# A selective-scan loop regrouped into pairs of chunks, with its preparation moved further ahead

## The chip, the cores and the metric

The kernel runs on one core of a Trainium2 chip. The metric is the device time of one execution in microseconds (us). The engines are named as the profile names them: PE (TensorE: matmuls and transposes; PEld is its weight loading), DVE (VectorE), ACT (ScalarE), POOL (GpSimd) and SP (SyncE, which here only issues DMA transfers). Each engine executes its own instructions strictly in the order in which the program lists them; engines wait for one another through semaphores. A difference of under 0.2% (3 us here) can't be told from no change by the runs of this kernel.

## The reference: what is computed

Two layers over a sequence of 1024 tokens, each with a width of 1024. The first is a gated MLP with a causal mixing over chunks of 128 tokens. The second, which the change touches, is a Mamba-2 mixer. Cut to what matters here, with G = 8 groups of J = 4 heads, chunks of 128 tokens, head size P = 64, state size N = 128:

```
proj = h @ w_in                                   # z, x, B, C and dt
xbc  = silu(causal_conv4(x, B, C) + bias)         # 4 taps along the tokens
cs   = cumsum(dt * A)                             # within a chunk
w_ls = (C @ B.T) * exp(cs_l - cs_s) * dt_s        # causal, 128 x 128, for each head
y_diag = w_ls @ x                                 # within the chunk
states = B.T @ (exp(cs_end - cs) * dt * x)        # what a chunk adds to the state
prev_c = prev_(c-1) * exp(cs_end) + states        # carried from chunk to chunk
y_off  = (C @ prev) * exp(cs)                     # from earlier chunks
y = y_diag + y_off + x * d_skip
out = rmsnorm_by_group(y * silu(z)) @ w_out
```

## The kernel before, in words

Everything is float32; big products run as three matmuls of a split into a high and a low part (`mm3`, L131 to L136). The order of all instructions is written out by hand: under `manual_schedule` the order of the Python calls is the order on each engine.

The last third of the kernel is one loop, `scans()` (L1854). It goes over 64 pieces n = 0..63, which are 8 groups g with 8 chunks c each. Two kinds of work are woven together on PE. One is the scan itself, with small matmuls. The other is filler: `project(want(..))` takes the next units of a generator that first computes the x, B, C and z columns that the second half of the groups still needs (128x512 matmuls into the PSUM tiles `ab`) and at the end begins the output product (`bo`). One unit is six matmuls. `want` (L1881) spreads the units evenly, 2.24 a chunk, half of them after the first stretch of the chunk and half after the second.

For a chunk, PE does two stretches of small matmuls:

- `pe_b` (L1620): y_off (two 128x128 matmuls with the carried state as weights, L1626), the chunk's own contribution to the state (128x256, L1633), and y_diag (four 128x128 matmuls, L1636). The y_diag matmuls use only 64 columns of the array each: two heads share the 128 partitions of the output, and the weights are 128x64. In every fourth chunk `sum_b` (L1702) follows, which sums squares for the norm, also with 64 columns. All of these write the PSUM tiles `yy` and `sp`.
- `pe_a` for the chunk two ahead (L1593, L1594): three transposes (x in two parts, B) and C @ B.T into the tile `tp`.

Around them: `load` brings the cumulative sums of a chunk to all partitions (tile `wl`, 256 KB, SP), `decay` turns them into exp(cs_l - cs_s) on ACT (L1599, L1601), `tokens` (DVE, ACT, POOL) reads `tp` into the tile `cw`, `weights` (DVE, L1617) multiplies `wl` by C @ B.T. `update` (DVE, L1656) and `carry` (POOL, L1647) form the state, `out` and `gate` the result. `queue` holds the steps of the convolution over the filler's products (one ACT pass, three DVE passes L1322 and a Silu for each `ab` tile); `drain()` runs one of them, once a chunk.

Half of the groups (0, 1, 3 and 5, `SPILT`) had their x, B, C computed earlier; they lie in DRAM as `xbc_d` and come back in halves of four chunks (1 MB each) through `prefetch` (L1549), which also loads z and exp(cs) (tile `ze`). SP issues all those transfers in program order, so a transfer waits behind the one before it. `prefetch(g, 1)` is called at the end of chunk 1 of group g, `prefetch(g + 1, 0)` at the end of chunk 5. The sums of squares go to DRAM through `sum_c` (`ss_d<-gsq`), called at the end of chunks 0 and 4, a chunk after `sum_b`.

PSUM has eight banks of 128x512; the `ab` tiles take four of them, and `yy`, `sp`, `tp` share the other four.

Of the kernel before, what the change touches and what calls it, by code (L numbers as in the profile page):

```python
# [11 lines left out]
ALU = mybir.AluOpType  # L12
# [3 lines left out]
P = 128  # L16
# [6 lines left out]
G = 8  # L23
# [6 lines left out]
def kernel(  # L30
# [21 lines left out]
    nc = tc.nc  # L52
# [1344 lines left out]
    def projections():  # L1397

        seq = [(g, kind) for g in plain for kind in ("x", "bc")] + [(G - 1, "z")]
        raw, W = {}, {}  # L1400

        def cols(g, kind):
            return ((g * 256, g * 256 + P) if kind == "z" else (DI + g * 256, DI + g * 256 + P) if kind == "x"
                    else (2 * DI + g * P, 2 * DI + 1024 + g * P))

        def load(i, kh):
            if i < len(seq):
                c = cols(*seq[i])
                r = slice(kh * 512, (kh + 1) * 512)
                raw[i, kh] = load_raw([b_w_in[r, k:k + P] for k in c] if seq[i][1] == "bc" else  # L1410
                                      [b_w_in[r, c[0]:c[0] + 256]], 4)

        def prep(i, kh):
            if i < len(seq):
                W[i, kh] = wh([P, 4, 256]), wl([P, 4, 256])
                split(*W[i, kh], raw.pop((i, kh)), nc.gpsimd if i else V)
                load(i + 1, kh)

        def push(g, kind, m, a):
            if m == 0:  # L1420
                sts[g][kind] = s8([P, 2, T], kind)
            if kind == "z":
                queue.append([lambda: nc.scalar.activation(sts[g][kind][:, m, :], a.rearrange("p a b -> p (a b)"),
                                                           AF.Silu)])
                return 1
            ops = conv_ops(sts[g][kind][:, m, :], a.rearrange("p a b -> p (a b)"), (cols(g, kind)[m] - DI) // P)
            n = len(queue)
            ops = [[o] for o in ops]
            if queue:
                queue[-1] += ops.pop(0)  # L1430
            queue.extend(ops)
            if m == 1:
                queue.append([lambda: nc.scalar.activation(sts[g][kind], sts[g][kind], AF.Silu)])
            return len(queue) - n

        for kh in range(2):
            load(0, kh)
        yield
        for kh in range(2):
            prep(0, kh)  # L1440
            yield
        last = 0
        for i, (g, kind) in enumerate(seq):
            for m in range(2):
                drain(len(queue) - last)
                ab = acc2("ab")
                for kh in range(2):
                    for th in (1, 0):
                        for k in range(4):
                            mm3(ab[:, th, :], [w[:, k, m * P:(m + 1) * P] for w in W[i, kh]],  # L1450
                                [h_[:, k, :] for h_ in H2[f"A{2 - th}{kh + 1}"]], kh == 0 and k == 0,
                                kh == 1 and k == 3)
                            if (kh, th, k) == (1, 0, 3):
                                last = push(g, kind, m, ab)
                            if k % 2:
                                yield
                    if (m, kh) == (0, 1):
                        prep(i + 1, 0)
                    elif (m, kh) == (1, 0):
                        prep(i + 1, 1)  # L1460
# [85 lines left out]
    ss_d = dr.tile([G, T], F32, name="ss_d")  # L1546
    rs_d = dr.tile([G, T], F32, name="rs_d")

    def prefetch(g, th):  # L1549

        st = sts[g]
        if g in xbc_d:
            t = st["xbc", th] = s8([P, 4, 512], "xbc")
            nc.sync.dma_start(out=t, in_=xbc_d[g][:, th])
        ze = st["ze", th] = s8([P, 4, 512], "ze")
        if g < G - 1:
            nc.sync.dma_start(out=ze[:, 0:2], in_=z_d[g][:, :, th * 512:(th + 1) * 512])
# [6 lines left out]
    class Scan:  # L1564


        def __init__(self, g, eng):
            self.g, self.st, self.eng = g, sts[g], eng
            self.wl, self.tp, self.cw, self.ps, self.state = {}, {}, {}, {}, {}
            if g < G - 1:  # L1570
                gd.append(dr.tile([P, 2, T], F32, name=f"g_d{g}"))
            else:
                gd.append(self.st["x"])
# [43 lines left out]
            V.tensor_tensor(out=wl, in0=wl, in1=self.cw[c][:, 640:768].unsqueeze(1).broadcast_to([P, 4, P]),  # L1617
                            op=ALU.mult)

        def pe_b(self, c, ends=None):  # L1620

            w, wl = self.cw[c], self.wl.pop(c)
            yy = sm("yy")
            if c > 0:
                for pt in range(2):
                    nc.tensor.matmul(out=yy[:, 256 + pt * P:384 + pt * P],  # L1626
                                     lhsT=self.state[c - 1][:, pt * P:(pt + 1) * P], rhs=self.x(3, c),
                                     start=True, stop=True)
            sp = None
            if c < 7 or ends is not None:  # L1630
                sp = sm("sp")
            if c < 7:
                nc.tensor.matmul(out=sp[:, 0:256], lhsT=w[:, 512:640], rhs=w[:, 256:512], start=True, stop=True)  # L1633
            for j in range(4):
                pt, f = j // 2, j % 2
                nc.tensor.matmul(out=yy[f * 64:(f + 1) * 64, pt * P:(pt + 1) * P], lhsT=w[:, j * 64:(j + 1) * 64],  # L1636
                                 rhs=wl[:, j, :], start=True, stop=True)
            if ends is not None:
                ends.sum_b(sp[:, 256:512], 2 if ends.g == G - 1 else 1)
            self.ps[c] = yy, sp  # L1640

        def carry(self, c):

# [7 lines left out]
        def update(self, c):  # L1651
            if c == 0:
                self.state[0] = k1([P, 256], "state")
                V.tensor_copy(out=self.state[0], in_=self.ps[0][1][:, 0:256])
            elif c < 7:
                V.tensor_tensor(out=self.state[c], in0=self.ps[c][1][:, 0:256], in1=self.state[c], op=ALU.add)  # L1656

        def y(self, c):

# [1 line left out]
                return self.z(c)  # L1661
            return self.cw[c][:, 768:1024].rearrange("p (m l) -> p m l", m=2)

        def out(self, c):
            yy, t2 = self.ps.pop(c)[0], self.y(c)
            if c > 0:
                t1 = k1([P, 2, P], "t1")
                V.tensor_tensor(out=t1, in0=yy[:, 256:512].rearrange("p (m l) -> p m l", m=2),
                                in1=self.st["ze", c // 4][:, 2:4, c % 4 * P:c % 4 * P + P], op=ALU.mult)
            for pt in range(2):  # L1670
                V.scalar_tensor_tensor(t2[:, pt, :], self.x(pt, c), dsk[:, 2 * self.g + pt:2 * self.g + pt + 1],
                                       yy[:, pt * P:(pt + 1) * P], ALU.mult, ALU.add)
            if c > 0:
                self.eng.tensor_tensor(out=t2, in0=t2, in1=t1, op=ALU.add)

        def gate(self, c):
# [173 lines left out]
    def scans():  # L1850
# [27 lines left out]
                    scan[g] = Scan(g, nc.gpsimd)  # L1878
                getattr(scan[g], f)(c, *a)

        prefetch(0, 0)  # L1881
        project(AHEAD // 2 + 1)
        while todo or late:
            convolve()
        for n in range(2):
            at("load", n)
        drain(1)
        for n in range(2):
            at("decay", n)
        drain(len(queue))  # L1890
        at("pe_a", 0), at("tokens", 0), at("weights", 0)
        drain(len(queue))
        project(AHEAD)
        at("pe_a", 1), at("tokens", 1), at("weights", 1)
        at("load", 2)
        for n, (g, c) in enumerate(chunks):
            if n == M + 3:
                drain(len(queue))
# [4 lines left out]
                end["scan"] = scan[G - 1]  # L1903
                bo.get("b", 0, 0, 0)
            p = g if c >= 4 else g - 1
            at("pe_b", n, scan[p] if c % 4 == 3 and p >= 0 else None)
            project(want(n + .5))
            at("pe_a", n + 2)
            if n > 0:
                at("weights", n + 1)  # L1910
            at("update", n)
            at("out", n)
            at("decay", n + 2)
            at("carry", n + 1)
            drain()
            at("tokens", n + 2)
            at("gate", n)
            if n >= N - 7:
                k = n - N + 7
                if k % 2:  # L1920
                    bo.prep(1, k // 2)
                else:
                    bo.ready(0, 0, k // 2)
            at("load", n + 3)
            th = 0 if c >= 4 else 1
            if p >= 0:
                sc = scan[p]
                if p == G - 1:
                    if c == 5:
                        sc.gate_half(th), sc.squares(th)  # L1930
                elif c % 4 == 0:
                    sc.squares(th)
                elif c % 4 == 1:
                    sc.store(th)
                    sc.sum_a()
            if c % 4 == 0 and n >= 8:
                scan[g - 1].sum_c(1 - th)
            if g > 0:
                if c == 5:
                    rs[g] = group_rstd(g - 1, 0, T)  # L1940
                elif c == 6:
                    rs[g][0]()
                elif c == 7:
                    rs[g][1]()
            if c == 0 and g > 1:
                rs[g - 1][2]()
            if c == 1:
                prefetch(g, 1)
            if c == 5 and g < G - 1:
                prefetch(g + 1, 0)  # L1950
            project(want(n + 1))
        sc = scan[G - 1]
        for k in (0, 1):
            bo.get("a", 0, 1, k)
        bo.get("b", 1, 0, 0)
        sc.sum_c(0), rs[G - 1][2]()
        bo.prep(1, 3)
        sc.gate_half(1), sc.squares(1)
        end["half"] = [group_rstd(G - 1, 0, 512)]
# [61 lines left out]
```

## Time and profile before

| | |
|---|---|
| median of 3 runs | 1514.28 us (1512.39 to 1514.48) |
| the profiled execution: its own time | 1512.85 us |
| its span, first to last instruction | 1511.1 us |
| PE busy | 1471.6 us, 97% |
| DVE, ACT, POOL busy | 1053.7 (70%), 783.3 (52%), 401.5 us (27%) |
| scan loop, first to last y_diag | 1018.4 to 1350.4 us |
| granted PE clock in the loop | 1.00 |

The profile is of one execution. Matmuls overlap one another on PE, so the duration of one is longer than the distance to the next; costs are read here as the distance from the start of one group of matmuls to the start of the next. In a timeline, rows of equal matmuls are merged, "x4" being four entries; a float32 128x128 matmul leaves two entries. "Idle" time before an instruction is put down to what released it; "issue" means that nothing the profile shows was waited for.

### The profile page before, as it was taken

What the parts mean: (1) busy time and instruction counts of PE and PEld (TensorE: products, weight loads), DVE (VectorE), ACT (ScalarE), POOL (GpSimd) and SP (SyncE); (2) the same over time, 40 slices, a digit from 0 to 9 for tenths busy, and PEclk for the clock granted to TensorE, in tenths of its full rate; (3) what the DMA queues carried; (4) which work ended last, traced back from release to release, by engine and by line L of the source; (5) the groups of instructions that cost most, each with busy time, mean ns of one, the idle gap of its engine ahead of it and who ended that gap; (6) DMA issues with size and microseconds to landing.
All of it is one profiled execution on the core that took longest, in us unless ns stands there. A gap on an engine that the chain in (4) does not pass through costs nothing. (4 is left out here: it accounts for less than half of the span.)

```text
span 1511.1 us, 21297 instructions
## 1 busy us (share of the span) xinstructions
PE 1471.6 (97%) x7834; PEld 1222.5 (81%) x7834; DVE 1053.7 (70%) x1713; ACT 783.3 (52%) x1256; POOL 401.5 (27%) x451
## 2 busy tenths in 40 slices
PE   6899999999999999999999999999999999999997
PEld 6899988888888888877878888877777777777875
DVE  7966567665666655678666467867677787688876
ACT  6533332222323445565565566666676666756463
POOL 1111110000000023202131222217576766633121
PEclk9999999999999999999999999999999999999999
DMA  5554322322222999957377978677655565579973
GB/s 183 141 168 140 106 97 103 117 103 103 101 79 96 337 262 246 258 145 162 104 174 154 208 154 167 142 242 209 183 160 183 160 187 141 169 255 275 255 156 112
DMA packets 174952, 254.45 MB, mean 168 GB/s; under 512 B 16400, under 2 KB 103168, under 8 KB 171648
## 3 DMA queue, kind: packets, MB, share of 16 engines
q1 hardware_dynamic: 124768, 168.93, 36.0%
q0 software_dynamic: 42448, 70.27, 23.2%
q10 hardware_dynamic: 7632, 13.90, 2.6%
q8 instruction: 62, 1.02, 0.3%
q14 instruction: 42, 0.34, 0.1%
HBM read 186.14 MB, written 51.18 MB: 157 GB/s over the span
## 5 line engine op out<-in xcount | busy, mean ns | idle before, releaser
L134 PE MATMUL acc<-hh,wh 128*128 128x512 f32 x868 | 339.9, 392 | 0.9 <-ACT u L296 0.9
L136 PE MATMUL acc<-hh,wl 128*128 128x512 f32 x868 | 338.4, 390 | 2.0 <-DVE wl L112 1.8
L135 PE MATMUL acc<-hl,wh 128*128 128x512 f32 x868 | 337.9, 389 | 0.0
L112 DVE TENSOR_TENSOR wl<-wr,wh 128x1024 fp32r<-128x1024 f32 (+1 forms) x96 | 114.3, 1193 | 118.3 <-ACT wh L111 118.1
L136 PEld LDWEIGHTS acc<-hh,wl 128*128 128x128 f32 x868 | 162.9, 188 | 37.9 <-DVE wl L112 3.7
L134 PEld LDWEIGHTS acc<-hh,wh 128*128 128x128 f32 x868 | 163.1, 188 | 34.9 <-ACT u L296 1.7
L135 PEld LDWEIGHTS acc<-hl,wh 128*128 128x128 f32 x868 | 163.1, 188 | 33.1
L296 ACT COPY u<-acc 128x512 f32<-128x512 f32 x115 | 66.8, 583 | 197.8 <-PE acc L136 197.7
L111 ACT CAST wh<-wr 128x1024 fp32r<-128x1024 f32 (+1 forms) x112 | 115.2, 1030 | 94.4 <-PE acc L135 56.9
L136 PE MATMUL acc<-wh,hl 128*128 128x256 f32 x448 | 129.2, 288 | 4.1 <-DVE hl L407 3.7
L134 PE MATMUL acc<-wh,hh 128*128 128x256 f32 x448 | 129.6, 289 | 2.9 <-DVE wh L418 1.3
L135 PE MATMUL acc<-wl,hh 128*128 128x256 f32 x448 | 128.5, 287 | 1.3 <-DVE wl L421 1.3
L134 PE MATMUL ab<-hh,wh 128*128 128x512 f32 x288 | 124.7, 433 | 1.2 <-DVE zt L999 0.7
L136 PE MATMUL ab<-hh,wl 128*128 128x512 f32 x288 | 113.2, 393 | 0.0
L135 PE MATMUL ab<-hl,wh 128*128 128x512 f32 x288 | 112.7, 391 | 0.0
L136 PEld LDWEIGHTS acc<-wh,hl 128*128 128x128 f32 x448 | 87.6, 196 | 5.4 <-DVE hl L407 4.4
L134 PEld LDWEIGHTS acc<-wh,hh 128*128 128x128 f32 x448 | 87.8, 196 | 3.8 <-ACT hh L400 1.6
L135 PEld LDWEIGHTS acc<-wl,hh 128*128 128x128 f32 x448 | 87.8, 196 | 1.7 <-DVE wl L421 1.5
L1599 ACT ACTIVATE wl<-wl,tk 128x128 f32<-128x128 f32 x256 | 81.6, 392 | 3.0 <-DMA wl<-cs_d 2.7
L649 POOL DMA_DIRECT2D y_d<-y x8 | 4.4, 549 | 290.8 <-DVE y L646 290.8
L135 PE MATMUL bo<-wl,xh 128*128 128x512 f32 x192 | 75.8, 395 | 3.8 <-DVE wl L742 2.1
L112 DVE TENSOR_TENSOR wl<-t,wh 128x1024 fp32r<-128x1024 f32 (+1 forms) x38 | 45.5, 1196 | 47.5 <-ACT wh L111 47.4
(317 smaller groups left out, 3250.6 us busy)
## 6 DMA issues: line engine op xcount, KB each, us to landing
wr<-in_a_w_in_dram SPq DMA_DIRECT2D x48, 512.0 KB, 3.6
wl<-cs_d SPq DMA_DIRECT2D x64, 256.0 KB, 3.6
wr<-in_b_w_in_dram SPq DMA_DIRECT2D x30, 512.0 KB, 7.4
wb<-in_a_w_out_dram SPq DMA_DIRECT2D x10, 1024.0 KB, 11.7
wb<-in_b_w_out_dram SPq DMA_DIRECT2D x10, 1024.0 KB, 11.1
wr<-in_b_w_in_dram SPq DMA_DIRECT2D x36, 256.0 KB, 5.9
v<-v_d SPq DMA_DIRECT2D x8, 1024.0 KB, 5.1
y_d<-y POOLq DMA_DIRECT2D x8, 1024.0 KB, 5.8
```

What stands on the lines that cost most here:

```text
L111: nc.scalar.copy(out=hi, in_=src)
L112: return (eng or nc.vector).tensor_tensor(out=lo, in0=src, in1=hi.bitcast(F32), op=ALU.subtract)
L134: nc.tensor.matmul(out=o, lhsT=l[0], rhs=r[0], start=start, stop=False, **kw)
L135: nc.tensor.matmul(out=o, lhsT=l[0], rhs=r[1], start=False, stop=False, **kw)
L136: nc.tensor.matmul(out=o, lhsT=l[1], rhs=r[0], start=False, stop=stop, **kw)
L296: nc.scalar.copy(out=self.u[n][:, i], in_=a)
L649: store = lambda: nc.gpsimd.dma_start(out=y_d[-1], in_=y)
L1599: nc.scalar.activation(wl[:, j, :], wl[:, j, :], AF.Relu, scale=-1.0, bias=tokc(2, c, self.g)[:, j:j + 1])
```

## The change

The loop goes in pairs of chunks. `pe_b` is split in three: `diagonal(c)` does y_diag of both chunks c and c + 1, eight matmuls in one stretch, into one PSUM bank; `own(c)` the chunk's contribution to the state; `off(c)` its y_off, these two into a tile `os`. In an even chunk PE does own, off, then the diagonal parts of the pair, and `sum_b` behind them in every second pair; in an odd chunk only own and off. `out` is split into `skip` (adds x * d_skip to y_diag, for both chunks of the pair in the even one) and the rest.

`pe_a` and `tokens` run three chunks ahead instead of two, `weights` two ahead instead of one, `decay` three ahead. The loads of `wl` come two at a time, right behind the diagonal stretch that frees their buffers. `sum_b` moves from the last chunk of a half group to the first chunk behind it, and `sum_c` into the same chunk. `drain()` is called twice a chunk instead of once, and the first step of a new convolution is put in front of the queue's last entry instead of behind it. `prefetch` is split: the 1 MB `xbc` is asked for at the end of chunks 0 and 4, `ze` at the end of chunks 1 and 5, as before.

```diff
@@ push
             if queue:
-                queue[-1] += ops.pop(0)
+                queue[-1][:0] = ops.pop(0)
...
@@ class Scan
-        def pe_b(self, c, ends=None):
...
+        def diagonal(self, c):
+
             yy = sm("yy")
+            for e in range(2):
+                w, wl = self.cw[c + e], self.wl.pop(c + e)
+                self.yy[c + e] = yy[:, e * 256:(e + 1) * 256]
+                for j in range(4):
+                    pt, f = j // 2, j % 2
+                    nc.tensor.matmul(out=self.yy[c + e][f * 64:(f + 1) * 64, pt * P:(pt + 1) * P],
+                                     lhsT=w[:, j * 64:(j + 1) * 64], rhs=wl[:, j, :], start=True, stop=True)
+
+        def own(self, c):
+
+            w = self.cw[c]
+            if c < 7:
+                self.os[c] = sm("os")
+                nc.tensor.matmul(out=self.os[c][:, 0:256], lhsT=w[:, 512:640], rhs=w[:, 256:512],
+                                 start=True, stop=True)
+
+        def off(self, c):
+
+            if c == 7:
+                self.os[c] = sm("os")
             if c > 0:
                 for pt in range(2):
...
@@ scans
-            at("pe_b", n, scan[p] if c % 4 == 3 and p >= 0 else None)
-            project(want(n + .5))
-            at("pe_a", n + 2)
-            if n > 0:
-                at("weights", n + 1)
-            at("update", n)
-            at("out", n)
-            at("decay", n + 2)
-            at("carry", n + 1)
-            drain()
-            at("tokens", n + 2)
-            at("gate", n)
+            if c % 2 == 0:
+                at("own", n), at("off", n)
+                at("diagonal", n)
+                if c % 4 == 0 and g > 0:
+                    scan[g - 1].sum_b()
+                elif n == N - 2:
+                    scan[g].sum_b(n=2)
+                at("load", n + 4), at("load", n + 5)
+                project(want(n + .5))
+                at("pe_a", n + 3)
+                at("update", n)
+                at("carry", n + 1)
+                at("weights", n + 2)
+                at("decay", n + 3)
+                at("skip", n)
+                at("out", n)
+                at("skip", n + 1)
+                drain()
+                at("tokens", n + 3)
+                at("gate", n)
+                if c % 4 == 0 and g > 0:
+                    scan[g - 1].sum_c(1 if c else 0)
+                drain()
+            else:
+                at("own", n), at("off", n)
+                project(want(n + .5))
+                at("pe_a", n + 3)
+                at("update", n)
+                at("carry", n + 1)
+                at("weights", n + 2)
+                at("out", n)
+                drain()
+                at("decay", n + 3)
+                at("tokens", n + 3)
+                at("gate", n)
+                drain()
...
-            at("load", n + 3)
...
-            if c == 1:
-                prefetch(g, 1)
-            if c == 5 and g < G - 1:
-                prefetch(g + 1, 0)
+            k = n + 4
+            if c % 4 < 2 and k < N:
+                prefetch(k // 8, k // 4 % 2, c % 4)
             project(want(n + 1))
```

On PE, at chunk 6 of group 2 before (`yy` holds y_off and y_diag, `sp` the own part, `ab` is filler, `tp` the transposes of a later chunk):

```order
L1626 MATMUL yy<-bc,state 128x128 x2
L1633 MATMUL sp<-cw 128x256
L1636 MATMUL yy<-wl,cw 64x128 x4
L134 MATMUL ab<-hh,wh 128x512
L135 MATMUL ab<-hl,wh 128x512
L136 MATMUL ab<-hh,wl 128x512
L134 MATMUL ab<-hh,wh 128x512
L135 MATMUL ab<-hl,wh 128x512
L136 MATMUL ab<-hh,wl 128x512
L1593 MATMUL tp<-ident,xbc 128x128 x3
L1594 MATMUL tp<-xbc 128x128
```

The same chunk now, an even one (`os` holds own and y_off):

```order
L1638 MATMUL os<-cw 128x256
L1647 MATMUL os<-bc,state 128x128 x2
L1630 MATMUL yy<-wl,cw 64x128 x8
L134 MATMUL ab<-hh,wh 128x512
L135 MATMUL ab<-hl,wh 128x512
L136 MATMUL ab<-hh,wl 128x512
L134 MATMUL ab<-hh,wh 128x512
L135 MATMUL ab<-hl,wh 128x512
L136 MATMUL ab<-hh,wl 128x512
L1595 MATMUL tp<-ident,xbc 128x128 x3
L1596 MATMUL tp<-xbc 128x128
```

The stretch has eight y_diag matmuls instead of four; the transposes are those of chunk 1 of group 3 instead of chunk 0. An odd chunk has no `yy` row any more; this is chunk 1 of group 3:

```order
L1638 MATMUL os<-cw 128x256
L1647 MATMUL os<-xbc,state 128x128 x2
L134 MATMUL ab<-hh,wh 128x512
L135 MATMUL ab<-hl,wh 128x512
L136 MATMUL ab<-hh,wl 128x512
L134 MATMUL ab<-hh,wh 128x512
L135 MATMUL ab<-hl,wh 128x512
L136 MATMUL ab<-hh,wl 128x512
L1595 MATMUL tp<-ident,xbc 128x128 x3
L1596 MATMUL tp<-xbc 128x128
```

Its transposes are those of chunk 4, the first readers of the second half of `xbc`; before, they stood in chunk 2. On SP's queue, around the load of that half (before; `g_d` is a store of results, `rs_d` of norm factors, `wr` filler weights):

```order
L1709 DMA ss_d<-gsq 2x256
L1730 DMA rs_d<-rvv 128x8
L120 DMA wr<-in_b_w_in_dram 128x4x256
L1588 DMA wl<-cs_d 128x512
L1693 DMA g_d_9103<-ze 256x1x512
L1554 DMA xbc<-xbc_d_6211 128x2048
L1557 DMA ze<-z_d_5290 128x2x512
```

And now:

```order
L1590 DMA wl<-cs_d 128x512 x2
L1720 DMA ss_d<-gsq 2x256
L1555 DMA xbc<-xbc_d_6211 128x2048
L120 DMA wr<-in_b_w_in_dram 128x4x256
L1704 DMA g_d_9027<-ze 256x1x512
L1741 DMA rs_d<-rvv 128x8
L1559 DMA ze<-z_d_5290 128x2x512
```

The load stands right behind the pair of `wl` loads and the `ss_d` write, and all three of those wait for work of the same chunk.

## Rows read from the trace of the kernel before

**Rows 1.** Busy us of PE, PEld, DVE, ACT, POOL in the loop, clock, DMA.
```profile
1018.40:1350.60 332.20, 328.96 (x2025) 255.02 (x2026) 246.63 (x513) 229.06 (x473) 221.34 (x249) 1.00 0.63 185
```
**Rows 2.** What PE waited for in the loop: us in total, times, longest.
```profile
PE yy L1626 <- DVE state L1656: 1.5, 3, 0.8
...
PE ab L134 <- DVE x L1322: 0.4, 1, 0.4
```
**Rows 3.** The same view, PE's weight loads.
```profile
PEld yy L1636 <- issue: 15.6, 47, 0.3
PEld ab L134 <- issue: 12.5, 58, 0.4
```
**Rows 4.** PE's timeline, an ordinary chunk: start us, us, work.
```profile
1130.38 0.60 PE L1626 MATMUL yy<-bc,state 128*128 128x128 f32 x4
1130.82 0.60 PE L1633 MATMUL sp<-cw 128*128 128x256 f32 x2
1131.35 0.66 PE L1636 MATMUL yy<-wl,cw 128*64 128x128 f32 x8
1131.94 0.50 PE L134 MATMUL ab<-hh,wh 128*128 128x512 f32 x1
...
1133.45 0.38 PE L1593 MATMUL tp<-ident,x 128*128 128x128 f32 x2
...
1133.92 0.48 PE L134 MATMUL ab<-hh,wh 128*128 128x512 f32 x1
```
**Rows 5.** The same, a chunk with the sum of squares.
```profile
1138.45 0.49 PE L1593 MATMUL tp<-ident,xbc 128*128 128x128 f32 x3
...
1140.91 0.66 PE L1636 MATMUL yy<-wl,cw 128*64 128x128 f32 x8
1141.40 0.60 PE L1702 MATMUL sp<-gsq,ones 128*64 128x256 f32 x4
1141.93 0.50 PE L134 MATMUL ab<-hh,wh 128*128 128x512 f32 x1
```
**Rows 6.** Entries of y_diag (min/median/max ns) and of own (busy us, mean ns).
```profile
L1636 PE MATMUL yy<-wl,cw x512: 272/273/324, 1018.4 to 1350.4; 128*64 128x128 f32 x171
...
L1633 PE MATMUL sp<-cw 128*128 128x256 f32 x112 | 33.4, 380 | 0.0
```
**Rows 7.** SP's timeline: when transfers were issued.
```profile
1128.62 0.82 SPq L1554 DMA_DIRECT2D xbc<-xbc_d  x1
1142.87 0.50 SPq L1709 DMA_DIRECT2D ss_d<-gsq  x1
```
**Rows 8.** DMA issues: KB each, median us from issue to landing; from the page, then the loop.
```profile
v<-v_d SPq DMA_DIRECT2D x8, 1024.0 KB, 5.1
...
wl<-cs_d SPq DMA_DIRECT2D x60, 256.0 KB, 3.6
...
xbc<-xbc_d SPq DMA_DIRECT2D x7, 1024.0 KB, 11.8
```
**Rows 9.** DVE in the loop by line: busy us, mean ns, idle before and its releaser.
```profile
L1617 DVE TENSOR_TENSOR wl<-wl,cw 128x512 f32<-128x512 f32 x63 | 57.0, 906 | 18.1 <-ACT wl L1601 14.8 <-ACT cw L1611 0.4
L1322 DVE SCALAR_TENSOR_TENSOR bc<-ab,par,bc 128x1023 f32<-128x1023 f32 (+2 forms) x24 | 30.6, 1276 | 10.5 <-ACT bc L1328 10.4
...
L1607 DVE TENSOR_TENSOR cw<-tp,tk 128x256 f32<-128x256 f32 x63 | 26.4, 419 | 15.3 <-PE tp L1594 15.2
L1668 DVE TENSOR_TENSOR t<-yy,ze 128x256 f32<-128x256 f32 x55 | 23.0, 418 | 6.8 <-PE yy L1636 4.9
L1656 DVE TENSOR_TENSOR state<-sp,state 128x256 f32<-128x256 f32 x48 | 20.2, 420 | 24.5 <-PE sp L1633 10.6 <-POOL state L1647 5.3 <-POOL ze L1678 4.6
L1671 DVE SCALAR_TENSOR_TENSOR cw<-xbc,dsk,yy 128x128 f32<-128x128 f32 x64 | 19.1, 339 | 0.0
```
**Rows 10.** ACT in the loop, the same columns.
```profile
L1706 ACT COPY gsq<-sp 1x256 f32<-1x256 f32 x28 | 10.1, 362 | 16.4 <-PE sp L1702 16.2
L1433 ACT ACT_TABLE_LOAD x8 | 10.3, 1283 | 0.1
```

More of the change, by code (lines that the diff above doesn't have):

```diff
@@ L1547, with prefetch @@
     rs_d = dr.tile([G, T], F32, name="rs_d")
-    def prefetch(g, th):
+    def prefetch(g, th, part):
         st = sts[g]
-        if g in xbc_d:
-            t = st["xbc", th] = s8([P, 4, 512], "xbc")
-            nc.sync.dma_start(out=t, in_=xbc_d[g][:, th])
+        if part == 0:
+            if g in xbc_d:
+                t = st["xbc", th] = s8([P, 4, 512], "xbc")
+                nc.sync.dma_start(out=t, in_=xbc_d[g][:, th])
+            return
         ze = st["ze", th] = s8([P, 4, 512], "ze")
@@ L1568, in __init__ @@
             self.g, self.st, self.eng = g, sts[g], eng
-            self.wl, self.tp, self.cw, self.ps, self.state = {}, {}, {}, {}, {}
+            self.wl, self.tp, self.cw, self.yy, self.os, self.state = {}, {}, {}, {}, {}, {}
             if g < G - 1:
@@ L1618, in weights @@
                             op=ALU.mult)
-        def pe_b(self, c, ends=None):
-            w, wl = self.cw[c], self.wl.pop(c)
+        def diagonal(self, c):
             yy = sm("yy")
+            for e in range(2):
[14 more added lines that the diff above has]
+                self.os[c] = sm("os")
             if c > 0:
                 for pt in range(2):
-                    nc.tensor.matmul(out=yy[:, 256 + pt * P:384 + pt * P],
+                    nc.tensor.matmul(out=self.os[c][:, 256 + pt * P:384 + pt * P],
                                      lhsT=self.state[c - 1][:, pt * P:(pt + 1) * P], rhs=self.x(3, c),
                                      start=True, stop=True)
[L1629 to L1640, printed above, removed]
         def carry(self, c):
@@ L1653, in update @@
                 self.state[0] = k1([P, 256], "state")
-                V.tensor_copy(out=self.state[0], in_=self.ps[0][1][:, 0:256])
+                V.tensor_copy(out=self.state[0], in_=self.os[0][:, 0:256])
             elif c < 7:
-                V.tensor_tensor(out=self.state[c], in0=self.ps[c][1][:, 0:256], in1=self.state[c], op=ALU.add)
+                V.tensor_tensor(out=self.state[c], in0=self.os[c][:, 0:256], in1=self.state[c], op=ALU.add)
         def y(self, c):
@@ L1662, in y, with skip @@
             return self.cw[c][:, 768:1024].rearrange("p (m l) -> p m l", m=2)
[L1664 to L1669, printed above, removed]
+        def skip(self, c):
+            yy, t2 = self.yy.pop(c), self.y(c)
             for pt in range(2):
@@ L1672, in out @@
                                        yy[:, pt * P:(pt + 1) * P], ALU.mult, ALU.add)
+        def out(self, c):
+            os, t2 = self.os.pop(c), self.y(c)
             if c > 0:
+                t1 = k1([P, 2, P], "t1")
+                V.tensor_tensor(out=t1, in0=os[:, 256:512].rearrange("p (m l) -> p m l", m=2),
+                                in1=self.st["ze", c // 4][:, 2:4, c % 4 * P:c % 4 * P + P], op=ALU.mult)
                 self.eng.tensor_tensor(out=t2, in0=t2, in1=t1, op=ALU.add)
@@ L1879, in at @@
                 getattr(scan[g], f)(c, *a)
-        prefetch(0, 0)
+        prefetch(0, 0, 0), prefetch(0, 0, 1)
         project(AHEAD // 2 + 1)
@@ L1884, in scans @@
             convolve()
-        for n in range(2):
+        for n in range(4):
             at("load", n)
@@ L1891, in scans @@
         at("pe_a", 0), at("tokens", 0), at("weights", 0)
+        at("pe_a", 1), at("tokens", 1), at("weights", 1)
         drain(len(queue))
         project(AHEAD)
-        at("pe_a", 1), at("tokens", 1), at("weights", 1)
-        at("load", 2)
+        at("decay", 2)
+        at("pe_a", 2), at("tokens", 2)
         for n, (g, c) in enumerate(chunks):
@@ L1928, in scans @@
                 if p == G - 1:
-                    if c == 5:
+                    if c == 4:
                         sc.gate_half(th), sc.squares(th)
@@ L1935, in scans @@
                     sc.sum_a()
-            if c % 4 == 0 and n >= 8:
-                scan[g - 1].sum_c(1 - th)
             if g > 0:
-                if c == 5:
+                if c == 6:
                     rs[g] = group_rstd(g - 1, 0, T)
-                elif c == 6:
+                elif c == 7:
                     rs[g][0]()
-                elif c == 7:
-                    rs[g][1]()
             if c == 0 and g > 1:
+                rs[g - 1][1]()
+            if c == 1 and g > 1:
                 rs[g - 1][2]()
-            if c == 1:
-                prefetch(g, 1)
-            if c == 5 and g < G - 1:
-                prefetch(g + 1, 0)
+            k = n + 4
+            if c % 4 < 2 and k < N:
+                prefetch(k // 8, k // 4 % 2, c % 4)
             project(want(n + 1))
@@ L1955, in scans @@
         bo.get("b", 1, 0, 0)
-        sc.sum_c(0), rs[G - 1][2]()
+        sc.sum_c(0), rs[G - 1][1](), rs[G - 1][2]()
         bo.prep(1, 3)
```

## The prediction

> **What bounds the kernel now.** I first read the busy time of the engines over the scan loop: of 332.2 us PE is busy 329.0, at full granted clock, while DVE, ACT and POOL have 246.6, 229.1 and 221.3 [rows 1]. So the loop lasts as long as PE's own list of work, and an edit counts only if it shortens that list or makes PE wait. Second, what PE waits for there: the named waits for the scan's DVE work are 1.5 us for the state and 0.4 us for the convolution that frees an `ab` bank [rows 2]. Little is to be had from waits. Third, the weight loads, where 47 loads of y_diag idle for "issue", 15.6 us in all, and 58 loads of the first filler matmul 12.5 us [rows 3]. That idle time is not in PE's busy time, so I went to PE's timeline to see what a stretch costs from start to start.
>
> **What the pairing saves.** In an ordinary chunk y_off starts at 1130.38, own at 1130.82, y_diag at 1131.35, and the filler at 1131.94 [rows 4]. Eight entries of y_diag last 0.66 us from the first start to the last end, and one entry lasts 0.273 [rows 4, 6], so the distance between entries is (0.66 - 0.27) / 7 = 0.055 us and eight of them are 0.44 us of work. Own has two entries that last 0.60 together and 0.38 each [rows 4, 6]; their distance is 0.22, hence 0.44 of work, yet y_diag starts 0.53 after it: 0.09 is lost in going from full-width to 64-column matmuls. From y_diag to the filler it is 0.59, so 0.15 is lost coming back. One y_diag stretch thus costs 0.44 + 0.24. A second chunk in the same stretch should add 0.44 alone. That `sum_b`, also 64 columns wide, begins 0.49 after y_diag [rows 5], and not 0.53 or 0.59, points the same way. The loop has 64 stretches, after the change 32: 32 x 0.24 = 7.7 us saved. From below: if the loss went with each matmul the saving would be 0. From above: idle weight loads of 15.6 / 47 + 12.5 / 58 = 0.55 a stretch [rows 3] give 17, but most of that lies under running matmuls. I take 7.7, which is the start-to-start distance itself.
>
> A rule speaks against it. In rows 3 only 47 of 512 loads idle, one for a stretch. The Trainium skill (TensorE: Matmul & The Clock Gate, Part 3, what overlaps and what doesn't) says that a weight load overlaps running matmuls only when its row group differs; all eight y_diag matmuls use all rows, so by it each would pay and the saving would be near 0. The trace doesn't bear that out.
>
> **What stays the same.** Number and size of the matmuls; an odd chunk keeps own and y_off in one stretch (0.89 us: 0.44 + 0.45), and the transposes keep theirs (0.47, from 1133.45 to 1133.92 [rows 4]). `sum_b` stands behind a 64-column stretch before and after.
>
> **Waits of the state and the banks.** y_off of chunk n + 1 needs `update(n)`. Before, PE had y_diag, two units and the transposes between own(n) and that, about 4 us; now 4.2 in an odd chunk and over 5 in an even one. On DVE, which is strictly in order, an even chunk has update 0.42, weights 0.91, skip four times 0.34, the y_off product 0.42, tokens 0.42 and a masked copy of at most as much, and up to two convolution steps of 1.28 [rows 9]: 6.6 us; an odd one 5.2. A pair on PE lasts 332.2 / 32 = 10.4 us [rows 1], and there are 24 convolution steps for B and C [rows 9] and as many for x, 48 for 64 chunks, so the 11.8 of a full pair comes in every other pair at most, and DVE's lag of up to 2 us stays within the slack. The doubled drain frees the `ab` banks earlier. Where `weights` now waits for `decay`, skip, the product, tokens and the convolution are queued behind it on DVE, and the next update; that is the half chunk of slack just named. I count the 1.9 us of waits [rows 2] as gone. New ones of that kind I can't see; I put 0.5 us down for them (0 to 4). The end of the loop keeps its order of filler and output product: 0 (-2 to +2).
>
> **What the earlier transposes cost.** This is the term that can undo the rest. `xbc` is asked for at the end of chunk 0 (or 4) and first read by the transposes in the middle of chunk 1 (or 5); before, these stood in the middle of chunk 2, and SP reached the load early: issued 1128.62, read without a wait at 1138.45 [rows 5, 7], 9.8 us later. Now three things stand ahead of the load in SP's queue that wait for the same chunk: the two `wl` loads, released by the y_diag stretch, and the `ss_d` write, released by ACT's two copies of the sums, 0.36 each [rows 10]. Count from the start of own in chunk 0. Own 0.44, y_diag 1.12, `sum_b` 0.44: 2.0. The `ss_d` write follows 0.94 later (from 1141.93 to 1142.87 [rows 5, 7]) and takes 0.5, with a gap of 0.15 behind it: the load is issued at 3.6. PE comes to the transposes after those 2.0, two units (1.51 [rows 4], and about 1.4 for the second, which follows filler), the transposes of chunk 3 (0.47), a unit (1.51), own and y_off (0.89) and a unit (1.51): 9.3, or 7.9 where one unit fewer falls there. Lead: 5.7, or 4.3. In chunk 4 y_off adds 0.45 on both sides.
>
> There are eight such loads, the first ahead of the loop. Four have a lead of 5.7; one (group 5, second half) 4.3; the two of the first group have no `sum_b` ahead: 5.3 and 6.7. How long do they take? The landing named for `xbc` is 11.8, for a transfer of the same size and shape earlier in the kernel 5.1 [rows 8], and the case above was under 9.8. Before, the store `g_d` (256x512 float32, 512 KB) stands right ahead of the load on the queue; now two `wl` loads of 256 KB do, issued two microseconds earlier and landing in 3.6 [rows 8]. So I take 6.0, nearer to the 5.1. Waits: 4 x 0.3 + 1.7 + 0.7 + 0 = 3.6. At one place two filler loads of 256 KB are queued right ahead (1.2 more), and at group 5 a Silu with two table loads of 1.28 [rows 10] stands ahead of the copies on ACT (1.1 more): 5.9 us. Bounds: 2.3 at 5.1 or less, and 4 x 6.1 + 7.5 + 6.5 + 5.1 + 2.3 = 46 at 11.8. Each microsecond of landing is worth 7 us here.
>
> **The sum.** -7.7 - 1.9 + 0.5 + 5.9 = -3.2 against the profiled execution's own 1512.85 (its span of 1511.1 and 1.75 around it, which stays): 1509.6. The median of the runs stands 1.4 above that execution, so as a median 1511.
>
> **Rivals.**
> - *The half of xbc comes late* (slower). Place: the first transposes of each half group that is read back. With a landing of 7.5 the waits are 4 x 1.8 + 3.2 + 2.2 + 0.8 + 2.3 = 15.7, and the sum is +6.6: 1521. It decides from a landing of 6.5 on, where the sum is zero; from 7.0 it is slower by over 0.2%. For it: the 11.8, and stores that now follow the load at once. Against it: the store that stood ahead of the load is gone from there.
> - *The loads are hidden after all* (much faster). Landing at 5.1 with no delay on ACT leaves 0 to 1: -9, or 1505. For it: the 5.1 of the like-shaped load. The Trainium skill (DMA: Bandwidth & Descriptors, anatomy of one DMA) fits 2.0 us plus the bytes over 436 GB/s, an estimate of 4.4 us for this load, which points the same way; the 11.8 and the 5.1 [rows 8] both lie above it.
> - *The pairing saves little*, because the loss goes with the matmuls or the first filler matmul pays it anyway: saving 2 instead of 7.7, sum +2.5, 1517. Against it: 47 idle loads, not 512.
> - *No change to speak of*: saving and late loads cancel, landing of 6.1 to 7.0, 1511 to 1517.
>
> **How the numbers follow.** The forecast and its near neighbours, 1507.5 to 1511.3: 0.30. Loads hidden: 0.20. Cancelling: 0.24. Loads late: 0.20. Small saving: 0.06, half of it within 0.2%. 0.2% is 3 us, about what a measurement of this kernel can tell from no change. That makes faster 0.50, same 0.27, slower 0.23. The range leaves out the late loads beyond a landing of 7.4 and savings beyond 10 us: 1504 to 1520.
>
> **What would show it.** Right: on PE's timeline y_diag of a pair takes about 1.0 to 1.1 us from start to the next work, with half as many idle first loads; own followed by y_off 0.89. The transposes of chunk 4 and of chunk 0 in groups 0, 1, 3 and 5 wait for `xbc<-xbc_d`, 0 to 2 us each, seven places, and nowhere else does PE wait for a transfer. Wrong: those waits sum to over 9 us, or a y_diag stretch of a pair lasts 1.3, or PE waits for `weights` or the state more than the 1.5 us of before.

## The result, and the profile after

The changed kernel takes 1521.23 us (median of 4 runs, 1520.27 to 1521.52), the kernel before 1514.25: ratio 1.0043, 95% interval 1.003 to 1.0055. It is 7.0 us slower, where 3 us faster was forecast; the rival "the half of xbc comes late" had said 1521. The profiled executions differ by 7.5 us (spans 1518.6 and 1511.1), and all of that arises in the scan loop.

First the loop by windows, with the columns of [rows 1], from the first y_diag to the last, and two short stretches inside it:

```profile
1019.01:1354.00 334.99, 316.89 (x2004) 259.89 (x2005) 239.54 (x506) 228.92 (x471) 220.88 (x247) 0.99 0.63 180
1074.70:1078.20 3.50, 3.41 (x11) 2.95 (x12) 0.62 (x2) 3.47 (x10) 1.52 (x3) 0.51 1.02 233
1248.80:1252.30 3.50, 3.50 (x12) 2.92 (x11) 0.62 (x2) 1.87 (x5) 2.01 (x3) 0.51 0.40 125
```

PE is now idle for 18 us of the loop, where it was idle for 3 [rows 1], and has 12 us less busy time. (The loop's end marks are not quite comparable: the last y_diag now stands one chunk, some 5 us, earlier. Over the whole execution PE is busy 1463.4 us instead of 1471.6.) So two things happened: PE's list became shorter, and PE came to wait. The last column but two is the granted clock: in the two short stretches it is at half, 1.2 instead of 2.4 GHz.

What PE waited for in the loop, the view of [rows 2]:

```profile
PE tp L1595 <- DMA xbc<-xbc_d: 15.5, 7, 2.9
PE tp L1595 <- ACT bc L1433: 1.0, 1, 1.0
PE bo L135 <- DVE wl L112: 1.0, 1, 1.0
PE bo L134 <- ACT wh L111: 0.3, 1, 0.3
```

The waits of before for the state and an `ab` bank are gone. In their place stand seven waits for `xbc`, at just the seven places that the prediction named. From start to start of the matmuls around them they cost a little more, 16.6 us. The weight loads, as in [rows 3], show the other side:

```profile
PEld ab L134 <- issue: 7.9, 30, 0.4
...
PEld yy L1630 <- issue: 2.3, 7, 0.3
```

47 idle loads of y_diag have become 7, and 58 of the filler 30: about one for a pair of chunks, no longer one for a chunk.

One of the seven places on PE's timeline, chunks 4 and 5 of group 1, in the columns of [rows 4]:

```profile
1063.60 0.59 PE L1638 MATMUL os<-cw 128*128 128x256 f32 x2
1064.12 1.09 PE L1630 MATMUL yy<-wl,cw 128*64 128x128 f32 x16
1065.05 0.60 PE L1713 MATMUL pr<-gsq,ones 128*64 128x256 f32 x4
...
1070.37 0.59 PE L1638 MATMUL os<-cw 128*128 128x256 f32 x2
1070.80 0.61 PE L1647 MATMUL os<-xbc,state 128*128 128x128 f32 x4
1071.16 0.47 PE L134 MATMUL ab<-hh,wh 128*128 128x512 f32 x1
...
1072.40 0.40 PE L136 MATMUL ab<-hh,wl 128*128 128x512 f32 x1
1074.79 0.87 PE L1595 MATMUL tp<-ident,xbc 128*128 128x128 f32 x3 [1.99 <-DMA xbc<-xbc_d]
...
1076.31 0.63 PE L135 MATMUL ab<-hl,wh 128*128 128x512 f32 x1
1076.74 0.63 PE L136 MATMUL ab<-hh,wl 128*128 128x512 f32 x1
```

And SP's list at that place, the view of [rows 7], with the named landings, the view of [rows 8]:

```profile
1064.82 2.04 SPq L1590 DMA_DIRECT2D wl<-cs_d  x2
1066.96 0.57 SPq L1720 DMA_DIRECT2D ss_d<-gsq  x1
1067.59 0.34 SPq L1555 DMA_DIRECT2D xbc<-xbc_d  x1
```
```profile
wl<-cs_d SPq DMA_DIRECT2D x60, 256.0 KB, 4.7
...
xbc<-xbc_d SPq DMA_DIRECT2D x7, 1024.0 KB, 6.4
```

PE is ready for the transposes at 1072.63 (1072.40 and a filler distance of 0.23) and starts them at 1074.79: `xbc` was asked for at 1067.59 and reached PE 7.2 us later. At the seven places it is 8.1, 8.5, 7.2, 8.0, 6.1, 6.9 and 5.9, 7.2 in the mean. Behind the wait the filler matmuls follow one another at 0.43 instead of 0.23: that is the half clock. From 1074.79 to 1078.31 it takes 3.5 us for what takes 1.9 elsewhere, 1.6 lost, and as much again at 1248.80.

### The profile page after: what moved, and what is told of

It is laid out like the page before. It is cut to its first block, busy times and chain, and to the rows that moved or that the text cites. A ratio compares the mean times of both kernels' runs of the same rounds, so it can differ in the third digit from the quotient of the medians.

```text
span 1518.6 us, 21342 instructions
## 1 busy us (share of the span) xinstructions
PE 1463.4 (96%) x7834; PEld 1230.3 (81%) x7834; DVE 1049.1 (69%) x1713; ACT 784.2 (52%) x1256; POOL 402.0 (26%) x451
## 6 DMA issues: line engine op xcount, KB each, us to landing
wb<-in_a_w_out_dram SPq DMA_DIRECT2D x10, 1024.0 KB, 11.8
```

## The experiments

The theory after the comparison: the seven late loads are the whole loss, and the pairing earns more than the 7.7 us of the prediction. The main rival: other waits stand behind those for `xbc`, from a preparation that runs three chunks ahead. The ratios are to the kernel before, run beside each.

| kernel | median us | ratio (95%) | PE's named wait for xbc |
|---|---|---|---|
| changed kernel | 1521.2 | 1.0043 (1.003 to 1.0055) | 15.5 |
| e1: xbc first in SP's list | 1502.1 | 0.991 (0.989 to 0.9929) | none |
| e2: e1 without the pairing | 1518.2 | 1.0024 (1.0012 to 1.0037) | none |
| e3: xbc ahead of the sums | 1522.7 | 1.0045 (1.0029 to 1.0061) | 14.8 |
| e4: pairing alone | 1551.8 | 1.0243 (1.022 to 1.0266) | 24.4 |
| e5: wl behind xbc | 1509.2 | 0.9955 (0.994 to 0.997) | 3.9 |
| e6: pairing alone, xbc first | 1517.7 | 1.0025 (1.0015 to 1.0035) | none |
| e8: e1 with one drain | 1503.6 | 0.9931 (0.9918 to 0.9944) | none |
| e9: one wl behind xbc | 1511.4 | 0.9979 (0.9969 to 0.999) | 6.2 |

**e1, the load of xbc first.** In chunks 0 and 4 it is asked for at the top of the chunk:

```diff
+            if c % 4 == 0 and n + 4 < N:
+                prefetch((n + 4) // 8, (n + 4) // 4 % 2, 0)
             if c % 2 == 0:
                 at("own", n), at("off", n)
...
-            if c % 4 < 2 and k < N:
-                prefetch(k // 8, k // 4 % 2, c % 4)
+            if c % 4 == 1 and k < N:
+                prefetch(k // 8, k // 4 % 2, 1)
```

> The 1 MB load of xbc stands first in SP's list of chunks 0 and 4, ahead of the two wl loads and the write of the sums; PE's order is unchanged. Theory (the late load is the whole loss): in the changed kernel PE's transposes wait 15.5 us by name for xbc in seven places, 16.6 by start-to-start distances, and the granted clock is at half for two stretches behind such waits (2.4 us). With some 4 us more lead these go: 1521.2 - 16.6 - 2.4 = 1502, up to 1505 if the load is still held up by its buffer; that beats both kernels, with no half clock left in the loop. Rival (the waits only stand where PE would have waited anyway, for tokens, weights or banks of a preparation three chunks ahead): other waits take their place and the time stays at 1516 to 1521.

It took 1502.13 us, 19.1 less than the changed kernel and 0.9% less than the one before. What PE waits for in the loop is now

```profile
PE bo L135 <- DVE wl L112: 2.2, 3, 1.0
PE tp L1595 <- ACT bc L1433: 1.0, 1, 1.0
PE bo L134 <- ACT wh L111: 0.3, 1, 0.3
```

and the clock is at 1.00 throughout the loop. 16.6 us of waits and 3.2 at the half clock make 19.8; 19.1 came back by the medians, 17.9 between the spans (1518.6 and 1500.7); the profiled e1 has a stretch of 3.4 us at the half clock of its own behind the loop, which accounts for 1.7 of the difference. No other wait of that size stood behind them: the rival falls. SP had the load out long before the chunk's own work (which starts at 1059.25 here):

```profile
1053.29 0.32 SPq L1555 DMA_DIRECT2D xbc<-xbc_d  x1
1060.47 1.50 SPq L1590 DMA_DIRECT2D wl<-cs_d  x2
```

**e2, the pairing undone in e1.**

```diff
-            yy = sm("yy")
-            for e in range(2):
+            if c % 2 == 0:
+                self.bank = sm("yy")
+            yy = self.bank
+            for e in range(1):
...
             else:
                 at("own", n), at("off", n)
+                at("diagonal", n)
...
+                at("skip", n)
                 at("out", n)
```

> e1_xbc_first with the pairing alone undone: y_diag of one chunk stands in each chunk, behind own and y_off, and the skip of the second chunk in the odd one. It gives the price of a y_diag stretch by itself. By the prediction a stretch taken away is worth 0.24 us, 32 of them 7.7 us: e2 is 7.7 slower than e1. By the start-to-start distances in the changed kernel (3.12 a pair before, 2.76 after) it is 0.36 a pair: 11.6 slower. Rival (the saving is small, since the loss goes with each matmul): 0 to 2 slower.

It is 16.0 us slower than e1 by the medians, 13.6 by the profiled executions. PE's timeline of one chunk in e2, to the second filler matmul:

```profile
1087.83 0.59 PE L1640 MATMUL os<-cw 128*128 128x256 f32 x2
...
1088.80 0.66 PE L1632 MATMUL yy<-wl,cw 128*64 128x128 f32 x8
1089.39 0.50 PE L134 MATMUL ab<-hh,wh 128*128 128x512 f32 x1
1089.72 0.40 PE L135 MATMUL ab<-hl,wh 128*128 128x512 f32 x1
```

and of a pair in e1, the odd chunk and then an even one:

```profile
1087.06 0.59 PE L1638 MATMUL os<-cw 128*128 128x256 f32 x2
...
1087.86 0.47 PE L134 MATMUL ab<-hh,wh 128*128 128x512 f32 x1
1088.17 0.39 PE L135 MATMUL ab<-hl,wh 128*128 128x512 f32 x1
...
1091.27 0.59 PE L1638 MATMUL os<-cw 128*128 128x256 f32 x2
...
1092.23 1.09 PE L1630 MATMUL yy<-wl,cw 128*64 128x128 f32 x16
1093.26 0.50 PE L134 MATMUL ab<-hh,wh 128*128 128x512 f32 x1
1093.60 0.40 PE L135 MATMUL ab<-hl,wh 128*128 128x512 f32 x1
```

Without the pairing two chunks cost 2 x 1.89 = 3.78; with it 1.11 + 2.33 = 3.44. That is 0.34 a pair, and it recurs pair after pair along the loop: 32 x 0.34 = 10.9 us. Most of the rest is two waits of e2, in the loop by name:

```profile
PE tp L1595 <- DVE state L1665: 2.5, 1, 2.5
PE tp L1595 <- ACT cw L1613: 1.0, 1, 1.0
```

With these 3.5 us, 14.4 are accounted for, between the 13.6 and the 16.0 that were measured. The price of a stretch read from the changed kernel (0.36, 11.6 in all) was nearly right, the rival of 0 to 2 is out.

**e3, the load only ahead of the write of the sums.** The call `prefetch(.., 0)` of chunks 0 and 4 stands before `sum_c`, behind the `wl` loads.

> The changed kernel with the load of xbc put ahead of the write of the sums in SP's list, still behind the two wl loads; all else is unchanged. It takes away only the wait for ACT's copies of the sums and the write, about 1.5 us of lead. Theory (lead against landing decides, microsecond for microsecond): six places have that write ahead of the load, so the waits fall by 6 x 1.0 to 1.5 = 6 to 9 us, and the half clock goes where the wait falls below about 1.5: 1510 to 1515. Rival (the transfer itself is what is slow, because the wl loads ahead of it and the stores behind share the queues, so an earlier issue only lengthens its landing): waits stay above 13, time 1518 to 1521.

1522.69 us, with 14.8 us of waits: the rival was right, though the time is 1.7 above its range. SP, and then PE, at the place shown above:

```profile
1070.54 0.80 SPq L1590 DMA_DIRECT2D wl<-cs_d  x2
1071.38 0.97 SPq L1555 DMA_DIRECT2D xbc<-xbc_d  x1
```
```profile
1069.32 0.59 PE L1638 MATMUL os<-cw 128*128 128x256 f32 x2
...
1080.25 0.52 PE L1595 MATMUL tp<-ident,xbc 128*128 128x128 f32 x3 [1.74 <-DMA xbc<-xbc_d]
```

The load is issued 2.06 us after own's start, in the changed kernel 3.99 (1067.59 less 1063.60). But it reaches PE 8.87 after the issue instead of 7.20, so nearly all of the lead is lost again. A landing counted from the issue is not a constant of the transfer. In the trace's packet records the first packet of `xbc` begins 3.5 to 4.1 us after its issue at all seven places of e3, and at the three of the changed kernel where loads were issued within 1.2 us ahead of it. At the other four, where the write of the sums and its wait lie between, the first begins after 1.0 us, but the last ends only after 5.4 to 6.4. At the place shown (1067.59) the packets of the two `wl` loads run until 2.6 us after the issue of `xbc`, and the first packet of a transfer behind it starts at 5.1, when most of `xbc` is through (its last packet ends at 6.3): of the rival's two reasons, the loads ahead and the stores behind, the records bear out the first.

**e4, the pairing alone.** Preparation, drains and order of the queue as before; `diagonal`, `skip`, `out` and `gate` of both chunks in the odd one:

```diff
+            at("own", n), at("off", n)
+            if c % 2:
+                at("diagonal", n - 1)
...
-                at("pe_a", n + 3)
+            at("pe_a", n + 2)
```

> The kernel before with the pairing alone: transposes two chunks ahead, one drain a chunk, one queue order and both parts of prefetch as before; y_diag of both chunks stands in the odd chunk behind its own and y_off, the skip, out and gate of both follow there. Theory (the pairing saves 0.24 to 0.36 us a pair and the preparation of the changed kernel adds only the late load): 1514.3 - 7.7 to 11.6 = 1503 to 1507, without a wait for xbc. Rival (without the preparation moved ahead the pair's DVE work comes too late, and PE waits for banks or weights in the odd chunk): 1510 or more, with new waits of PE for DVE.

1551.83 us, far above the theory's range. As a number it fits the rival's "1510 or more", but the largest wait is not the rival's. The theory's premise, that without the earlier transposes no wait for `xbc` would arise, is wrong:

```profile
PE tp L1595 <- DMA xbc<-xbc_d: 24.4, 7, 5.6
PE pr L1713 <- ACT gsq L1700: 4.3, 1, 4.3
```

Here the `wl` load and the store `g_d` that stand ahead of `xbc` on SP's list are released by the work of a whole pair, and the named landing of `xbc` is 9.2 us. The second of the seven loads, for one, is issued at 1046.91, and PE needs it 5 us later; in the kernel before there were 9.8 [rows 5, 7]. The late load is thus no matter of the transposes' place alone: the pairing moves the releases of what is queued ahead of it.

**e5, the two wl loads behind xbc.** It was made to test a new theory: the transfer waits in the DMA queue for those asked for before it.

```diff
-                at("load", n + 4), at("load", n + 5)
+                if c % 4:
+                    at("load", n + 4), at("load", n + 5)
...
                 prefetch(k // 8, k // 4 % 2, c % 4)
+            if c % 4 == 0:
+                at("load", n + 4), at("load", n + 5)
```

> The changed kernel with xbc asked for where it is, still behind the write of the sums, but with the two wl loads of chunks 0 and 4 put behind it on SP's list; they were ahead. In e3_xbc_before_ss_d an issue 1.9 us earlier after own brought the data no earlier, which the prediction's sum (lead against a fixed landing) doesn't allow. New theory (the transfer waits in the DMA queue until the two wl loads of 256 KB before it are through, and then takes 3 to 4 us itself): with nothing ahead, xbc issued within 0.5 us of where it was lands some 4 us later instead of 7.2; the waits fall from 15 to 0 to 4, the half clock goes, and the time is 1502 to 1507. Rival (the transfer is slow by itself, or shares the engines with the store and the loads behind it): landing stays at 6 to 7, waits at 10 to 15, the time at 1516 to 1522.

The waits fell from 15.5 to 3.9 us, as the theory had it; the time, 1509.2, is 2 above its range. SP and PE at the same place:

```profile
1061.49 0.57 SPq L1720 DMA_DIRECT2D ss_d<-gsq  x1
1062.12 0.34 SPq L1555 DMA_DIRECT2D xbc<-xbc_d  x1
1062.57 0.85 SPq L1590 DMA_DIRECT2D wl<-cs_d  x2
```
```profile
1058.58 0.59 PE L1638 MATMUL os<-cw 128*128 128x256 f32 x2
...
1067.61 0.49 PE L1595 MATMUL tp<-ident,xbc 128*128 128x128 f32 x3
```

The load goes out 3.54 us after own's start, within 0.5 of the changed kernel, and 5.5 us later PE needs it and doesn't wait. By the packet records its last packet ends 4.7 us after the issue, at the five places with this order of events 4.6 to 4.8, where the changed kernel shows 5.4 to 7.4. The other two places, in group 0, are no test of the theory: no write of the sums stands there, so without the `wl` loads ahead of it `xbc` goes out much earlier (1016.59 for 1020.70, and 1032.33 for 1043.94, of which 3 are the shift of the loop itself), and that alone can explain why their 5.6 us of waits are gone. At the five the waits fall from 9.8 to 3.9. Of these, 3.5 are at group 5, where the write of the sums itself comes late. The prediction had named a Silu ahead of ACT's copies; what stands right ahead of them is a decay that waits 1.20 us for its `wl` load and takes a table load of 1.28 with it, and then a cast of filler weights:

```profile
1224.88 1.28 ACT L1601 ACTIVATE wl<-wl,tk 128x128 f32<-128x128 f32 x4 [1.20 <-DMA wl<-cs_d]
```

The half clock follows that wait of PE too (0.50 from 1235.5 to 1240.5).

The Trainium skill (DMA: Bandwidth & Descriptors, Queues, rings and completion order) says that on each DMA engine the descriptors of one queue are consumed in ring order. e3 and e5 agree: only a place ahead of the `wl` loads brought the data earlier, an earlier issue behind them did not.

**e9, one wl load ahead, one behind.** The edit is half of that of e5.

> Between the changed kernel (two wl loads of 256 KB ahead of xbc on SP's list) and e5_wl_behind_xbc (none): one wl load ahead of the write of the sums and xbc in chunks 0 and 4, the other behind. xbc reached PE 7.2 us after its issue with two ahead, and about 4.4 with none. Theory (xbc's packets start when those of the wl loads before it are through): about 5.8 with one, which leaves waits of 0 to 2 us at the places with the least lead and 3 to 4 at group 5's second half, 5 to 9 in all; time 1509 to 1514. Rival (a store or another transfer is what holds it up, and the order of wl matters only through SP's own time): landing within 0.5 us of one of the two ends, waits about 4 or about 15, time as e5 (1509) or as the changed kernel (1521).

1511.41 us, 6.2 us of waits in five places, the longest 3.2 at group 5: within what the theory said. The named landings of `xbc` in the loop, first of e9, then of e5 (6.4 in the changed kernel):

```profile
xbc<-xbc_d SPq DMA_DIRECT2D x7, 1024.0 KB, 5.5
```
```profile
xbc<-xbc_d SPq DMA_DIRECT2D x6, 1024.0 KB, 5.2
```

Waits of 15.5, 6.2 and 3.9 us with two, one and no `wl` load ahead: the dose has its effect. At the five places outside group 0 alone they are 9.8, 4.8 and 3.9, and the last packet of `xbc` ends 6.2, 5.3 and 4.7 us after the issue in the mean.

**e6, the pairing alone with xbc first.** e4, with the load as in e1 and the last `sum_b` of the loop at the end of its chunk.

> e4_pairing_alone (transposes two chunks ahead, one drain a chunk) with xbc first on SP's list of chunks 0 and 4, and the last sum of squares of the loop asked for at the end of its chunk, where ACT has long formed its input. It tells whether the preparation three chunks ahead is needed at all. In e4 37 us were lost, 24.4 of them by name at xbc, 4.3 at the last sum, and several at the half clock behind such waits. Theory (the pairing earns 11 us, and the rest was the late load): 1503 to 1508. Rival (with the preparation two ahead the pair's work on DVE and ACT comes too late): PE's waits for DVE, ACT and POOL, 6.2 us by name in e4, stay or grow, and the time is 1509 to 1520.

1517.68 us: the rival was right. No wait for `xbc` is left, but PE waits, among others, for

```profile
PE pr L1713 <- ACT gsq L1700: 2.9, 1, 2.9
...
PE os L1638 <- DVE t L1683: 1.3, 3, 0.5
```

The 2.9 are due to this experiment: I put that sum where its input still wasn't ready. Behind it the granted clock is 0.59 from 1350.8 to 1354.8. By the starts of the same filler matmuls e6 loses about 7 of its 15 us against e1 around that place; the rest is many waits of 0.5 to 1.1 for DVE, ACT and POOL. So the preparation further ahead is not what costs in the change. That the pairing needs it is likely, but no run shows it by itself: e6 also has the skip, out and gate of both chunks in the odd one, and one drain with the old order of the queue (1.5 us in e8, below).

**e8, one drain a chunk and the old order of the queue, in e1.** `drain()` is taken out once in each branch, and `queue[-1][:0] = ..` becomes `queue[-1] += ..` again.

> e1_xbc_first with one drain a chunk instead of two, and the first step of a convolution behind the queue's last entry as before: these two parts of the change undone. Theory (they only order work off the critical path; the waits for banks were 0.4 us before): within 2 us of e1, 1500 to 1504. Rival (with DVE's extra work in even chunks the banks come free too late): waits of ab for DVE and ACT appear, 1505 or more.

1503.6 us, 1.5 above e1, as expected, and no more than the runs can tell from no change. These two parts are worth little.

## Why the prediction was wrong, step by step

- *The stretches*: 7.7 forecast, 10.9 measured (e1 and e2). A pair's y_diag takes 0.93 us ahead of `sum_b` and 1.03 ahead of filler, as forecast. What was missed is the odd chunk: own followed by y_off lasts 0.79 up to the filler (1070.37 to 1071.16), not 0.89. The 0.89 came from rows in which other small matmuls follow; straight ahead of filler y_off takes 0.36 (1070.80 to 1071.16), not 0.45. So a stretch of y_diag costs 0.10 beyond the 0.24 of the forecast. The rival "saves little" is out, and of the weight loads only 7 of y_diag idle. The Trainium skill (TensorEngine Tiling (Array Packing), Key Properties) says that a change of tiling mode drains the engine. e1 against e2 agrees: 0.34 us for entering and leaving once, and that per stretch, not per matmul.
- *The waits of state and banks*: gone, as forecast. New: 1.0 for a Silu in the last group, and a few tenths at `bo`; 0.5 was put down.
- *The issue of the load*: forecast 3.6 us after own's start, measured 3.99. *PE's need*: forecast 9.3, measured 9.03 (1072.63 less 1063.60). The lead was 5.0 instead of 5.7, both errors small and in the same direction.
- *The landing of 6.0* is the step that failed. PE got the data 7.2 us after the issue. With a landing of 7.2 and leads 0.7 shorter, the prediction's own terms give 4 x 2.2 + 3.6 + 2.6 + 1.2 = 16.2, without its two extra delays, which the measured 7.2 holds already; 16.6 were measured. (The 7.2 is a mean of landings from 5.9 to 8.5, so the agreement is rough.) The prediction had named the two `wl` loads right ahead of `xbc`, and priced them at nothing beyond SP's own time, since they were "issued two microseconds earlier and landing in 3.6". They land in 4.7 now that two come together, and `xbc` comes through behind them. The 5.1 of [rows 8] was of a load with a free queue: e5, with a free queue, shows 5.2. The fit that the prediction cites from the Trainium skill (DMA: Bandwidth & Descriptors, Anatomy of one DMA) is given there for transfers that GpSimd issues. SP issues this load, and with no other load ahead its last packet ends 4.6 to 4.8 us after the issue, against the estimate of 4.4. Nor was 11.8 the landing in the kernel before: by the packet records its seven loads ended 5.3 to 11.2 us after their issue, 7.3 in the median, and PE waited at none of them. So 6.0 would have been too short even there, and the term was 16.6 and not 5.9.
- *The half clock* wasn't foreseen: 3.2 us behind two of the seven waits.

Together: -10.9 - 1.9 + 1.5 + 16.6 + 3.2 = +8.5, measured 7.5 between the spans. The rival that came true had the right place and almost the right sum of waits (15.7), though its saving was too small and the half clock was missing. That its 1521 is the measured time is partly luck: the 3.2 us that it saved too little and the 3.2 at the half clock cancel. One sum of the prediction is off without consequence: DVE's work in an even chunk adds up to 6.5, not 6.6.

## What to carry to other kernels

Price a load from where it stands in its queue, not from the median landing of its like: here what was asked for right ahead of it cost up to 2.7 us (last packet after 7.4 instead of 4.7), and an issue 1.9 us earlier behind the same neighbours brought next to nothing (e3). When work is regrouped, list each queue anew with what releases each entry, and put the large load that the critical engine needs ahead of small ones that are needed later. The matmuls that use half of the array's columns paid 0.34 us once for a stretch, so gathering such groups pays as long as their inputs come in time (e1, and not e4 or e6).

## What the hardware showed unexpectedly

After a wait of PE the granted clock can fall to half: in the changed kernel behind 2 of its 7 waits (2.0 and 2.9 us by name), for 3.5 us and at a cost of 1.6 each, and not behind two others just as long (2.9 and 2.8; the stretches from 1028.80 and from 1052.40, right behind them, show 1.00). In e3 it came at the first of these places too, behind a wait of 2.8 (0.66 from 1029.6 to 1034.6), and in e1 behind one of 1.75 past the loop (0.50 from 1363.5 to 1366.9). The length of the wait alone doesn't decide it; what does is left open.
